# Weight sums and alpha*h rows moved between VectorE and GpSimd in a hybrid S5 and gMLP encoder layer

## The chip, the core and the metric

The kernel runs on one core of a Trainium2 chip. The metric is the time of one execution in microseconds of the device, and the time of a kernel is the median of its runs. The profile is of one further execution. TensorE does the matrix products, VectorE and GpSimd do elementwise work, ScalarE does activations and copies, and the queues of SyncE and ScalarE issue the transfers between device memory and the on-chip buffers.

## The reference

One layer of width 1024 over 2048 positions, all in float32, with `D_FF` 2816 and `ALPHA` the fourth root of 2:

```
h = layer_norm(x, emb_ln_g, emb_ln_b)
z = h @ w_in
y_ssm = s5_mixer(z[..., :512], ...)          # diagonal state space layer, GELU, GLU
y_sgu = sgu_mixer(z[..., 512:], ...)         # gated mixing inside blocks of 128 positions
mix = concat([rms_norm(y_ssm), rms_norm(y_sgu)]) @ w_out
h = layer_norm(ALPHA * h + mix, ln1_g, ln1_b)
ffn = (silu(h @ w_gate) * (h @ w_up)) @ w_down
ple = (p @ w_ple) * sigmoid(h @ w_ple_gate + b_ple_gate)
h = layer_norm(ALPHA * h + ffn + ple, ln2_g, ln2_b)
```

## The kernel before

Every product of float32 matrices is made of three passes. An operand is split into a rounded high part, which ScalarE casts (line 64), and the low rest, which VectorE subtracts (line 65); `mm3` then issues high times high (line 69), high times low (line 70) and low times high (line 71), each with 512 columns. So a tile of weights is usable after a load, a cast on ScalarE and a subtraction on VectorE. Raw loads go through three buffers (`raw`), split weights through six (`wsp`), and the pools `hT` and `hTx` hold 14 tiles each.

The work that the change touches lies between the end of the GLU and the start of the gated feed-forward network.

`glu` ends with the scaled rows of the state space branch (line 912), which are stored to `md`. Before its last step it starts the first output projection, `out_proj(0)`, which multiplies four tiles of 128 rows by the left half of `w_out`. When `glu` is done, its memory is freed, and the pool `pb` of `phase_b` is laid over it.

`mixed` then goes over four sets `tg` of 512 rows. For each set it loads the normalized input rows into four tiles `acc` (eight exist), scales them (line 1043), adds the output projection of two column halves (line 1061), takes the statistics (line 116), normalizes in place (line 299), and lets TensorE transpose eight column blocks (line 143). ScalarE writes the transposed rows with gain and bias (line 1071) to `hfd`. After that GpSimd turns the four `acc` tiles into `alpha*h`: for each column half it multiplies by `ALPHA*ln1_g` (line 1083) and adds `ALPHA*ln1_b` (line 1084), 16 instructions a set, from one buffer `S` that is loaded for each half and scaled by ScalarE (line 1080). SyncE stores the result to `xnd` (line 1086). The output projection of set `tg+1` is issued inside set `tg`, so that TensorE has work while VectorE normalizes. The split tiles of `w_out` are kept for all four sets: `keep` gives 14 tiles of `hTx` and two of `ff`.

Between the sets, `gate_sums` makes for one or two of four row groups the four sums of blocks of `w_ple_gate` that a seven-product scheme (Strassen and Winograd) needs: four loads into `tx` (line 1110; six tiles exist), four GpSimd instructions (lines 1111 to 1114) and four stores to `pgd` (line 1116). `operands(0)` loads the first block of transposed rows (block 0 is sets 0 and 1, block 1 is sets 2 and 3), splits it, and makes for each of four `j` the sums of it on GpSimd (`sums_B`, lines 1347 to 1350). `ple` runs the seven products of the gate of the per-layer embedding; product 2 and later ones read the sums, and its results go into eight new `acc` tiles (line 1199), whose memory is that of the sets' tiles once these are stored. Set 3 is cut in two: the first half is before the first products of `ple`, the statistics and everything after them follow its second product.

Then each of the two blocks runs 11 steps of `gate` and `up` (seven products each, with weight sums on GpSimd in `ops_A`, lines 1362 to 1369), and the products of `down`. In these steps `residual` reads `xnd` back and adds it to the accumulators on GpSimd (line 1243), two tiles a step in eight of the steps. In block 0 the steps also hold `down_sums`, four GpSimd instructions each (lines 1126 to 1129).

Each engine executes its own instructions in the order that a planner wrote before the run: it walks through the program by priority (earlier in the program goes first) and puts on each engine what is ready by its own estimate of durations. In the run, an engine or a queue whose next instruction waits does not go past it.

Of the kernel before, what the change touches and what calls it, by code (L numbers as in the profile page):

```python
# [7 lines left out]
F32 = mybir.dt.float32  # L8
# [3 lines left out]
ALU = mybir.AluOpType  # L12

P = 128
# [10 lines left out]
ALPHA = 2.0 ** 0.25  # L25
# [25 lines left out]
class Kern:  # L51
# [903 lines left out]
    def w_out(self, hf, k, t0):  # L955


        if (hf, k) not in self.wres:
            src = self.a["w_out"][0].rearrange("(k p) c -> p k c", p=P)
            k0 = k - k % 2  # L960
            r = self.load_w(src[:, k0:k0 + 2, hf * 512:(hf + 1) * 512], 1024)
            for i in range(2):
                w = self.keep() if hf or t0 else self.wspt()
                self.split(w[:, 0], w[:, 1], r[:, i * 512:(i + 1) * 512])
                self.wres[hf, k0 + i] = w
        return self.wres[hf, k] if hf or t0 else self.wres.pop((hf, k))

    def keep(self):
        self.kept += 1
# [3 lines left out]
    def phase_b(self, ctx):  # L973
        pb = self.pb = ctx.enter_context(self.tc.tile_pool(name="pb", bufs=1))
        a = self.a
        w_g = a["w_ffn_gate"][0].rearrange("(k p) c -> p k c", p=P)
        w_u = a["w_ffn_up"][0].rearrange("(k p) c -> p k c", p=P)
        mixed = self.mixed()
        for tg in range(3):
            next(mixed)  # L980
            self.gate_sums((tg, 3) if tg == 0 else (tg,))
        B = self.operands(0)
        next(B)
        next(mixed)
        tail = iter(())
        for blk in range(2):
            accs = [[None] * 4, [None] * 4]
            ple = self.ple(blk, B, accs)
            if blk == 0:
                next(ple)  # L990
                for _ in B:
                    pass
                next(ple)
                for _ in mixed:
                    pass
            for _ in ple:
                next(tail, None)

            rest = self.residual(blk, accs)
            for i in range(NP):  # L1000
                f = self.gate(w_g, i, self.B)
                if i:
                    next(rest, None)
                if blk == 0:
                    self.down_sums(i)
                self.up(blk, w_u, i, self.B, f)
            B = self.operands(1) if blk == 0 else iter(())
            tail = self.norm_out(blk, accs)
            for _ in self.down(blk, accs, tail):
                next(B, None)  # L1010
            for _ in B:
                pass
        for _ in tail:
            pass

    def mixed(self):


        nc, a = self.nc, self.a
        v = nc.vector  # L1020
# [16 lines left out]
        for tg in range(4):  # L1037
            c0 = tg * 512
            acc = []
            for t in range(4):  # L1040
                x = self.acct()
                nc.sync.dma_start(out=x, in_=self.h0d[c0 + t * P:c0 + (t + 1) * P, :])
                v.tensor_tensor(out=x, in0=x, in1=ag0, op=ALU.mult)
                acc.append(x)
            if tg == 0:
                op, ps0 = self.op0, self.op0_ps
                bias(ps0, 0)
                cps = [self.t512() for _ in range(4)]
                for t in range(4):
                    nc.scalar.copy(out=cps[t], in_=ps0[t])  # L1050
                pss = [cps, bias(next(op), 1)]
            else:
                pss = [bias(next(nxt), 0), ps1]
            if tg < 3:
                nxt = self.out_proj(c0 + 512)
                next(nxt)
                ps1 = bias(next(nxt), 1)
            for hf in ((0, 1) if tg == 0 else (1, 0)):
                for t in range(4):
                    xs = acc[t][:, hf * 512:(hf + 1) * 512]  # L1060
                    v.tensor_tensor(out=xs, in0=xs, in1=pss[hf][t], op=ALU.add)
            if tg == 3:
                yield
            mv = self.ln_stats(acc, D)
            rs = self.ln_rstd(mv)
            for t in range(4):
                self.normalize(acc[t], mv[:, t, 0:1], rs[:, t:t + 1])
            for k in range(8):
                ps = self.transpose4(acc, k * P)
                f = self.t512()  # L1070
                nc.scalar.activation(out=f, in_=ps, func=AF.Identity, scale=self.g1[:, k:k + 1],
                                     bias=self.b1[:, k:k + 1])
                nc.scalar.dma_start(out=self.hfd[tg, k * P:(k + 1) * P, :], in_=f)

            for hf in range(2):
                cs = slice(hf * 512, (hf + 1) * 512)
                gb = self.stile()
                for i, nm in enumerate(("ln1_g", "ln1_b")):
                    nc.sync.dma_start(out=gb[:, i], in_=a[nm][0][cs].unsqueeze(0).broadcast_to([P, 512]))
                nc.scalar.mul(gb, gb, ALPHA)  # L1080
                for t in range(4):
                    xs = acc[t][:, cs]
                    nc.gpsimd.tensor_tensor(out=xs, in0=xs, in1=gb[:, 0], op=ALU.mult)  # L1083
                    nc.gpsimd.tensor_tensor(out=xs, in0=xs, in1=gb[:, 1], op=ALU.add)  # L1084
            for t in range(4):
                nc.sync.dma_start(out=self.xnd[c0 + t * P:c0 + (t + 1) * P, :], in_=acc[t])
            yield

    def operands(self, blk):

        B = self.B = [[None] * 4 for _ in range(7)]
        for k in range(8):
            B[k // 4][k % 4] = self.split_f(self.load_f(blk, 0, k), self.hxt())
            if k == 3 and blk:
                yield
        yield
        for j in range(4):
            B[2][j] = self.split_f(self.load_f(blk, 1, j + 4), self.hxt())
            self.sums_B(blk, B, j)
            if blk:  # L1100
                yield

    def gate_sums(self, kks):

        g = self.nc.gpsimd
        W = self.a["w_ple_gate"][0].rearrange("(j k p) c -> k p j c", j=2, p=P)
        for kk in kks:
            a11, a12, a21, a22 = x = [self.txt() for _ in range(4)]
# [123 lines left out]

    def residual(self, blk, accs):

        for tg in range(2):
            for t in range(4):
                for hf in range(2):
                    cs = slice(hf * 512, (hf + 1) * 512)
                    x = self.txt()
                    r0 = blk * 1024 + tg * 512 + t * P  # L1240
                    self.nc.sync.dma_start(out=x, in_=self.xnd[r0:r0 + P, cs])
                    xs = accs[tg][t][:, cs]
                    self.nc.gpsimd.tensor_tensor(out=xs, in0=xs, in1=x, op=ALU.add)
                yield

    def rows(self, src, scale):

# [278 lines left out]
```

## Time and profile before

| | |
|---|---|
| median of 3 runs | 2327.17 us (2325.92 to 2329.01) |
| the profiled execution | 2327.55 us, with a span of 2325.8 us |
| TensorE matmul busy | 2171.2 us (93% of the span) |
| VectorE busy | 1555.5 us (67%) |
| ScalarE busy | 879.7 us (38%) |
| GpSimd busy | 734.6 us (32%) |
| mean granted TensorE clock | 0.97 |

The profiled execution is 1.75 us longer than its span; the sums further down are made against its own time. PE is TensorE, DVE is VectorE, ACT is ScalarE, POOL is GpSimd, and SPq, ACTq are queues that issue transfers. A busy share is an average over stages with different limits, so the stage around the change is read by itself.

### The profile page before, as it was taken

What the parts mean: (1) busy time and instruction counts of PE and PEld (TensorE: products, weight loads), DVE (VectorE), ACT (ScalarE), POOL (GpSimd) and SP (SyncE); (2) the same over time, 40 slices, a digit from 0 to 9 for tenths busy, and PEclk for the clock granted to TensorE, in tenths of its full rate; (3) what the DMA queues carried; (4) which work ended last, traced back from release to release, by engine and by line L of the source; (5) the groups of instructions that cost most, each with busy time, mean ns of one, the idle gap of its engine ahead of it and who ended that gap; (6) DMA issues with size and microseconds to landing.
All of it is one profiled execution on the core that took longest, in us unless ns stands there. A gap on an engine that the chain in (4) does not pass through costs nothing.

```text
span 2325.8 us, 27952 instructions
## 1 busy us (share of the span) xinstructions
PE 2171.2 (93%) x9556; PEld 1768.9 (76%) x9556; DVE 1555.5 (67%) x2672; ACT 879.7 (38%) x1503; POOL 734.6 (32%) x650
## 2 busy tenths in 40 slices
PE   7899998998799789999999989989999999999996
PEld 6677887766677567888888768868788888878885
DVE  7997779787465646666666676574566666565559
ACT  4434554442223433323232444434333332324442
POOL 1187100002535514645454330043134343410004
PEclk9999999999899899999999999989999999999998
DMA  8547445546765343454544666643233333336563
GB/s 265 148 141 244 122 136 155 147 127 232 254 238 200 128 138 133 166 173 166 173 167 164 227 212 209 196 151 130 82 105 127 106 126 116 107 130 214 194 197 134
DMA packets 312427, 382.66 MB, mean 165 GB/s; under 512 B 62246, under 2 KB 180054, under 8 KB 312284
## 3 DMA queue, kind: packets, MB, share of 16 engines
q1 hardware_dynamic: 261116, 315.30, 42.1%
q10 hardware_dynamic: 50080, 61.36, 7.5%
q0 software_dynamic: 1088, 4.21, 0.5%
q8 instruction: 75, 1.23, 0.2%
q14 instruction: 68, 0.56, 0.1%
HBM read 270.16 MB, written 110.64 MB: 164 GB/s over the span
## 4 chain that ended last, share of the span: by engine, by line
PE 65%; DVE 13%; DMA 7%; issue 7%; POOL 6%; ACT 1%; SPq 1%; POOLq 0%; ACTq 0%; DVEq 0%
PE ps L69 21%; PE ps L70 21%; PE ps L71 21%; DVE st L116 2%; POOL acc L1083 1%; DMA tx<-hfd 1%; POOL acc L1084 1%; DVE wsp L65 1%; PE ps L143 1%; DMA raw<-in_w_out_dram 1%; DVE hTx L65 1%; DVE z L912 1%; DMA raw<-in_w_ple_gate_dram 1%; POOL acc L1292 1%; DMA raw<-md 0%
## 5 line engine op out<-in xcount | busy, mean ns | idle before, releaser
L65 DVE TENSOR_TENSOR wsp<-raw,wsp 128x512 fp32r<-128x512 f32 x459 | 395.3, 868 | 293.4 <-ACT wsp L64 287.9
L64 ACT CAST wsp<-raw 128x512 fp32r<-128x512 f32 x469 | 287.6, 622 | 550.1 <-PE ps L71 320.0
L69 PE MATMUL ps<-hT,wsp 128*128 128x512 f32 x744 | 290.8, 391 | 6.1 <-ACT hT L312 6.1
L70 PE MATMUL ps<-hT,wsp 128*128 128x512 f32 x744 | 290.6, 391 | 1.0 <-DVE hT L313 1.0
L71 PE MATMUL ps<-hT,wsp 128*128 128x512 f32 x744 | 290.3, 390 | 0.0
L69 PE MATMUL ps<-wsp,ff 128*128 128x512 f32 x636 | 254.0, 399 | 20.9 <-ACT ff L64 20.9
L71 PE MATMUL ps<-wsp,ff 128*128 128x512 f32 x636 | 252.6, 399 | 5.6 <-DVE ff L65 5.4
L70 PE MATMUL ps<-wsp,ff 128*128 128x512 f32 x636 | 253.2, 398 | 0.2 <-DVE wsp L65 0.2
L69 PE MATMUL ps<-hTx,wsp 128*128 128x512 f32 x616 | 241.0, 391 | 3.7 <-DVE tx L1395 3.7
L70 PE MATMUL ps<-hTx,wsp 128*128 128x512 f32 x616 | 239.8, 389 | 0.0
L71 PE MATMUL ps<-hTx,wsp 128*128 128x512 f32 x616 | 239.7, 389 | 0.0
L1362 POOL TENSOR_TENSOR S<-raw 128x512 f32<-128x512 f32 x44 | 68.3, 1553 | 388.5 <-DVE wsp L65 279.4
L64 ACT CAST wsp<-S 128x512 fp32r<-128x512 f32 x158 | 97.9, 620 | 240.5 <-PE ps L71 164.3
L70 PE MATMUL ps<-wsp,hT 128*128 128x512 f32 x400 | 159.2, 398 | 15.0 <-DVE wsp L65 15.0
L69 PE MATMUL ps<-wsp,hT 128*128 128x512 f32 x400 | 160.7, 402 | 7.4 <-ACT acc L1199 5.5
L69 PEld LDWEIGHTS ps<-hT,wsp 128*128 128x128 f32 x744 | 140.3, 189 | 35.4 <-ACT hT L312 6.5
L70 PEld LDWEIGHTS ps<-hT,wsp 128*128 128x128 f32 x744 | 140.2, 188 | 31.0 <-DVE hT L313 2.3
L71 PEld LDWEIGHTS ps<-hT,wsp 128*128 128x128 f32 x744 | 140.2, 188 | 29.1
L1292 POOL TENSOR_TENSOR acc<-acc,t 128x512 f32<-128x512 f32 x24 | 36.3, 1530 | 399.1 <-ACT acc L1286 399.1
L65 DVE TENSOR_TENSOR wsp<-S,wsp 128x512 fp32r<-128x512 f32 x158 | 122.8, 777 | 56.5 <-ACT wsp L64 54.3
L69 PEld LDWEIGHTS ps<-wsp,ff 128*128 128x128 f32 x636 | 122.7, 193 | 49.4 <-ACT ff L64 24.0
L71 PE MATMUL ps<-wsp,hT 128*128 128x512 f32 x400 | 158.3, 396 | 0.0
(342 smaller groups left out, 4344.4 us busy)
## 6 DMA issues: line engine op xcount, KB each, us to landing
raw<-fod SPq DMA_DIRECT2D x126, 256.0 KB
raw<-in_w_in_dram SPq DMA_DIRECT2D x48, 512.0 KB
raw<-in_w_ffn_gate_dram SPq DMA_DIRECT2D x44, 512.0 KB
raw<-in_w_ffn_up_dram SPq DMA_DIRECT2D x44, 512.0 KB
fod<-tx ACTq DMA_DIRECT2D x88, 256.0 KB
raw<-wtd SPq DMA_DIRECT2D x72, 256.0 KB
fod<-ff ACTq DMA_DIRECT2D x66, 256.0 KB
tx<-hfd SPq DMA_DIRECT2D x56, 256.0 KB
```

Of the source, the lines that this page charges most:

```text
L64: nc.scalar.copy(out=hi, in_=src)
L65: (e or nc.vector).tensor_tensor(out=lo, in0=src, in1=hi.bitcast(F32), op=ALU.subtract)
L69: mm(ps, lhsT=lh, rhs=rh, start=start, stop=False, skip_group_check=more)
L70: mm(ps, lhsT=lh, rhs=rl, start=False, stop=False, skip_group_check=more)
L71: mm(ps, lhsT=ll, rhs=rh, start=False, stop=stop, skip_group_check=more)
L116: nc.vector.bn_stats(out=st[:, c, :], in_=t[:, c * 512:(c + 1) * 512])
L143: self.nc.tensor.transpose(ps[:, t * P:(t + 1) * P], x[:, col:col + P], self.ident)
L912: v.scalar_tensor_tensor(out=mx[:, ct, :].rearrange("p (c s) -> p s c", s=L), in0=yT[ct].rearrange("p (s c) -> p s c", s=L), scalar=self.g ...
L1083: nc.gpsimd.tensor_tensor(out=xs, in0=xs, in1=gb[:, 0], op=ALU.mult)
L1084: nc.gpsimd.tensor_tensor(out=xs, in0=xs, in1=gb[:, 1], op=ALU.add)
L1292: nc.gpsimd.tensor_tensor(out=xh, in0=xh, in1=gb[0][hf], op=ALU.mult)
L1362: g.tensor_tensor(out=s1, in0=a21, in1=a22, op=ALU.add)
```

## The change

It has five parts.

1. `gate_sums` runs its four sums on VectorE instead of GpSimd, 16 instructions in all.
2. In `mixed`, sets 0 and 1 have their gain and bias (32 instructions) on VectorE. Sets 2 and 3 have none: their normalized rows are stored to `xnd` as they are, without the loads into `S`.
3. `residual` of block 1 makes up for it: in each of its eight steps it loads gain and bias for 512 columns into an `ff` tile, scales them on ScalarE, and multiplies and adds on GpSimd before the addition that was there. The steps go over two row tiles and one column half each, in place of one row tile and two halves.
4. `operands` yields after each `j` in both blocks, and `phase_b` takes one more step of it, so that the split and the sums for `j` 0 stand in the program before set 3.
5. Of the right half of `w_out`, the tiles `k` 4 to 7 are split into `wsp` for set 0 and not kept. Set 1 loads and splits them again and keeps them. `keep` still hands out 16 tiles.

```diff
-                w = self.keep() if hf or t0 else self.wspt()
+                w = self.keep() if t0 or (hf and k < 4) else self.wspt()
...
-        return self.wres[hf, k] if hf or t0 else self.wres.pop((hf, k))
+        return self.wres[hf, k] if t0 or (hf and k < 4) else self.wres.pop((hf, k))
...
         B = self.operands(0)
         next(B)
+        next(B)
         next(mixed)
...
-            for hf in range(2):
+            for hf in range(2 if tg < 2 else 0):
...
-                    nc.gpsimd.tensor_tensor(out=xs, in0=xs, in1=gb[:, 0], op=ALU.mult)
-                    nc.gpsimd.tensor_tensor(out=xs, in0=xs, in1=gb[:, 1], op=ALU.add)
+                    v.tensor_tensor(out=xs, in0=xs, in1=gb[:, 0], op=ALU.mult)
+                    v.tensor_tensor(out=xs, in0=xs, in1=gb[:, 1], op=ALU.add)
...
             self.sums_B(blk, B, j)
-            if blk:
-                yield
+            yield
...
     def gate_sums(self, kks):
-        g = self.nc.gpsimd
+        g = self.nc.vector
...
     def residual(self, blk, accs):
+        nc, g, a = self.nc, self.nc.gpsimd, self.a
         for tg in range(2):
-            for t in range(4):
+            for t0 in (0, 2):
                 for hf in range(2):
                     cs = slice(hf * 512, (hf + 1) * 512)
-                    x = self.txt()
-                    r0 = blk * 1024 + tg * 512 + t * P
-                    self.nc.sync.dma_start(out=x, in_=self.xnd[r0:r0 + P, cs])
-                    xs = accs[tg][t][:, cs]
-                    self.nc.gpsimd.tensor_tensor(out=xs, in0=xs, in1=x, op=ALU.add)
-                yield
+                    if blk:
+                        gb = self.fft(F32)
+                        for i, nm in enumerate(("ln1_g", "ln1_b")):
+                            nc.sync.dma_start(out=gb[:, i],
+                                              in_=a[nm][0][cs].unsqueeze(0).broadcast_to([P, 512]))
+                        nc.scalar.mul(gb, gb, ALPHA)
+                    for t in (t0, t0 + 1):
+                        x = self.txt()
+                        r0 = blk * 1024 + tg * 512 + t * P
+                        nc.sync.dma_start(out=x, in_=self.xnd[r0:r0 + P, cs])
+                        if blk:
+                            g.tensor_tensor(out=x, in0=x, in1=gb[:, 0], op=ALU.mult)
+                            g.tensor_tensor(out=x, in0=x, in1=gb[:, 1], op=ALU.add)
+                        xs = accs[tg][t][:, cs]
+                        g.tensor_tensor(out=xs, in0=xs, in1=x, op=ALU.add)
+                    yield
```

## Rows read from the trace of the kernel before

**Rows 1.** Windows: us, busy PE, PEld, DVE, ACT, POOL (xcount); PEclk, DMA share, GB/s.

```profile
530.00:890.00 360.00, 305.76 (x1301) 242.81 (x1301) 209.66 (x304) 119.41 (x191) 150.26 (x107) 0.91 0.58 197
...
540.00:600.00 60.00, 49.02 (x216) 38.94 (x214) 50.82 (x64) 17.75 (x30) 24.48 (x15) 0.93 0.72 249
...
890.00:1298.00 408.00, 404.29 (x1771) 331.37 (x1771) 264.27 (x335) 130.91 (x216) 207.58 (x140) 1.00 0.49 163
...
1660.00:2088.00 428.00, 427.93 (x1886) 353.92 (x1884) 266.18 (x358) 135.93 (x223) 147.86 (x100) 1.00 0.34 111
```

**Rows 2.** TensorE's waits, 530 to 890 us: us in total, times, longest us.

```profile
PE ps L143 <- ACT t L1071: 11.4, 1, 11.4
PE ps L70 <- DVE wsp L65: 9.6, 3, 8.4
PE ps L69 <- ACT hTx L64: 7.4, 1, 7.4
PE ps L143 <- DVE acc L299: 7.3, 8, 3.7
PE ps L69 <- ACT acc L1199: 5.5, 3, 4.1
PE ps L143 <- DVE acc L1190: 5.2, 1, 5.2
```

**Rows 3.** Timeline of TensorE (start us, us, what): first and last of ten matmuls.

```profile
537.50 0.77 PE L69 MATMUL ps<-hTx,hT 128*128 128x512 f32 x1 [7.40 <-ACT hTx L64]
...
541.60 0.40 PE L69 MATMUL ps<-hTx,hT 128*128 128x512 f32 x1
```

**Rows 4.** Timeline of SyncE's queue, five of its rows.

```profile
524.86 1.04 SPq L266 DMA_DIRECT2D raw<-in_w_out_dram  x2
...
576.65 4.47 SPq L1116 DMA_DIRECT2D pgd<-tx  x4
...
582.21 1.44 SPq L266 DMA_DIRECT2D raw<-in_w_out_dram  x3
...
625.35 7.00 SPq L1086 DMA_DIRECT2D xnd<-acc  x4
632.44 2.41 SPq L944 DMA_DIRECT2D raw<-md  x3
```

**Rows 5.** Timeline of GpSimd: second weight sums, first and last; end of set 0's rows.

```profile
572.96 1.29 POOL L1111 TENSOR_TENSOR tx<-tx 128x512 f32<-128x512 f32 x1 [6.68 <-DMA tx<-in_w_ple_gate_dram]
...
578.08 2.22 POOL L1114 TENSOR_TENSOR tx<-tx 128x512 f32<-128x512 f32 x1
...
629.47 2.53 POOL L1084 TENSOR_TENSOR acc<-acc,S 128x512 f32<-128x512 f32 x2
```

**Rows 6.** Timeline of ScalarE: casts before line 1071 and after the sums; a late copy.

```profile
599.11 0.62 ACT L64 CAST hT<-raw 128x512 fp32r<-128x512 f32 x1 [1.88 <-DMA raw<-md]
...
778.10 0.62 ACT L64 CAST hTx<-tx 128x512 fp32r<-128x512 f32 x1 [1.05 <-POOL tx L1350]
...
821.74 1.07 ACT L1199 COPY acc<-ps 128x512 f32<-128x512 f32 x2 [3.49 <-DMA xnd<-acc]
```

**Rows 7.** Timeline of VectorE: the same instruction alone, beside GpSimd, and late.

```profile
530.13 3.97 DVE L912 SCALAR_TENSOR_TENSOR z<-yT,chv,ps 128x512 f32<-128x512 f32 x4 [1.88 <-PE ps L909]
...
549.90 2.48 DVE L65 TENSOR_TENSOR hTx<-raw,hTx 128x512 fp32r<-128x512 f32 x4
...
588.88 10.12 DVE L65 TENSOR_TENSOR hTx<-raw,hTx 128x512 fp32r<-128x512 f32 x6 [0.89 <-ACT hTx L64]
...
637.88 1.43 DVE L65 TENSOR_TENSOR hT<-raw,hT 128x512 fp32r<-128x512 f32 x2 [10.76 <-ACT hT L64]
```

**Rows 8.** GpSimd by line (L1243: block 1): busy us, mean ns, idle before, releasers.

```profile
L1083 POOL TENSOR_TENSOR acc<-acc,S 128x512 f32<-128x512 f32 x32 | 45.9, 1455 | 60.7 <-PE ps L143 46.0 <-ACT S L1080 14.7
...
L1243 POOL TENSOR_TENSOR acc<-acc,tx 128x512 f32<-128x512 f32 x16 | 23.8, 1507 | 44.8 <-DMA tx<-xnd 44.8
...
L1111 POOL TENSOR_TENSOR tx<-tx 128x512 f32<-128x512 f32 x4 | 5.1, 1283 | 41.5 <-DMA raw<-md 21.7 <-DMA tx<-in_w_ple_gate_dram 10.0 <-DMA hfd<-t 9.8
```

## Prediction

> **What bounds the kernel now.** I read the windows first, to see which stretch TensorE loses, then its waits there, then the timelines of the queues that it waited on.
>
> TensorE is busy for 427.93 of 428 us in block 1's steps, but only for 305.76 of 360 us between the end of the GLU and the feed-forward network [rows 1]. These 54.2 us of idleness are almost all that this change can reach. Six kinds of wait hold 46.4 of them [rows 2]. Idleness costs a little more than itself: the granted clock is 0.91 in this stretch against 1.00 in the steps [rows 1], and after the wait of 7.4 us ten matmuls start within 4.10 us, nine intervals of 0.456 us [rows 3], where a full stretch has 428/1886 = 0.227 us [rows 1]. That is the lower of the two clock levels, and 9 x 0.229 = 2.1 us lost after one long wait.
>
> Traced back, the waits lead to GpSimd and to the SyncE queue that waits for it.
>
> - 7.4 us: set 0's second half needs split weights in `hTx`, memory that is free only when the GLU is through. Their loads were issued at 524.86 [rows 4], 12.6 us before TensorE starts at 537.50 [rows 3].
> - 11.4 us: set 0's transposes wait for line 1071 on ScalarE, which stands behind a cast at 599.11 that waited for a load [rows 6]. The loads of `w_out` before it left at 582.21, behind four stores of weight sums [rows 4], whose last GpSimd instruction ended at 580.30 [rows 5].
> - 7.3 us: the normalizations of sets 1 and 2. For set 1, VectorE stood still for 10.76 us before a split [rows 7]; its load left at 632.44, behind stores of `alpha*h` [rows 4] whose rows GpSimd finished at 632.00 [rows 5].
> - 9.6 and 5.2 us: `ple` waits for a weight split behind the last sums of `operands`, cast at 778.10 right after line 1350 [rows 6], and for set 3's normalization, behind those sums' splits on VectorE.
> - 5.5 us: copies into `acc` wait for the store of set 3's `alpha*h` [rows 2, 6].
>
> **The change, part by part.** *Durations.* On GpSimd an instruction of the moved kind takes 1.455 us [rows 8]. VectorE's subtraction, of the same shape and with two on-chip inputs, takes 2.48/4 = 0.62 us alone and 10.12/6 = 1.69 us beside GpSimd [rows 7]. I take 0.62 for moved work, since GpSimd then has little left beside it; 1.69 is the other bound.
>
> The Trainium skill (Perfetto Trace Analysis, Optimizing Scalar/DVE Operations) warns that moving work between VectorE and GpSimd might not help, because they share an SBUF read port. The rows show the sharing (0.62 against 1.69 us), but also that the work takes less than half as long on VectorE; by the rule the sum would be the 2311.6 of the first rival, by the rows it is the one below.
>
> *Weight sums (1) and set 0's first half (5).* The second set's four sums fall from 7.34 us (572.96 to 580.30 [rows 5]) to 4 x 0.62 = 2.5, and the first set's, at the mean, from 4 x 1.455 = 5.8 to 2.5. Both lie in the chain of loads, sums, stores and loads of `w_out`: 4.8 + 3.3 = 8.1 us earlier. The last load of `w_out` follows the second of the six subtractions that took 1.69 us each beside GpSimd: 2 x 1.07 = 2.1 more. So line 1071 comes 10 us sooner. TensorE's own arrival moves by enough: with weights in `wsp` it need not wait for 537.5, only for the first subtraction behind line 912, which ends at 534.1 [rows 7], or earlier, and then 48 x 0.227 = 10.9 us of products cover the time until the memory is free. Bounds: 0, if the loads are as late as now; 7.4 + 11.4 + 2 x 2.1 = 23.0, if both waits vanish. I take **10**, the shorter chain's.
>
> VectorE must hold it: it is busy for 50.82 of 60 us there [rows 1]. Added are 8 sums and 16 rows of set 0 (24 x 0.62 = 14.9 us, some after 600) and four splits (2.5); the subtractions freed from GpSimd give back 6.4 us and others like them more. It stays near full, which is why I don't take more than 10.
>
> *Rows of sets 0 and 1 on VectorE (2).* 16 x 1.455 = 23.3 us on GpSimd become 9.9 on VectorE, so the stores of `xnd`, and the loads that are queued behind them, leave some 10 us sooner; that covers VectorE's 10.76 us, and with it the normalizations' wait: 7.3 + 2.1 at most, 0 at least. I take **7**. The wait for the gain buffer (line 1080) moves to VectorE; queued behind it are splits, line 1061 and the next statistics, on which TensorE waits.
>
> *No rows for sets 2 and 3, and an earlier `j` 0 (2, 4).* GpSimd's 23.3 us of set 2 lie among its sums, which end that much sooner; TensorE comes 17 us sooner, so 6.3 of the 8.4 us wait go. Part 4 puts `j` 0's five loads, casts and subtractions and four sums ahead of set 3's on SyncE, ScalarE, VectorE and GpSimd; the splits end before set 3's statistics, and the 5.2 go. With half a slow clock after them, 1.5: **13**, from 5 to 14.8 + 2.1 = 16.9. Set 3's store leaves right after its transposes instead of behind 23.3 us of rows: 5.5 + 2.1 at most, **6**, at least 0. Four loads into `S` are saved on SyncE.
>
> *Block 1's residual (3).* 32 more GpSimd instructions of 1.507 us [rows 8], 48 us, in a GpSimd that is busy for 147.86 of 428 us [rows 1]. No TensorE wait is visible there now. Each step also issues two gain loads on SyncE, ahead of `ops_A`'s weight loads, and a scaling on ScalarE, ahead of casts that feed TensorE. Block 0, with `down_sums`' four instructions beside its residual's two, is the nearest row with six a step: 408/1771 against 428/1886 is 0.2304 against 0.2269 us a matmul, 0.58 us in a step of 168. Eight steps: 4.7 at most, 0 at least; I take **2**, as there are two fewer loads and stores of 512 KB than `down_sums` has.
>
> *Reload (5).* Two loads of 512 KB, 1.05 MB, at 197 GB/s [rows 1] are 5.3 us if nothing hides them; four casts and splits stand beside 21.8 us of products (96 x 0.227). I take **1**; 0 to 5.3.
>
> *Sum.* Against the profiled execution's 2327.55 us (span 2325.8 and 1.75 around it; 0.4 above the median of the runs): 10 + 7 + 13 + 6 = 36 gained, 3 lost, 2327.55 - 33 = **2294.6 us**. All bounds together: 2327.55 - 56.9 = 2271 and 2327.55 - 5 + 10 = 2333.
>
> **The rivals.** *VectorE inherits the waits (22%).* Sets 0 and 1 gain nothing, because VectorE now stands where GpSimd stood and its other work stands behind it; the 10 and the 7 are lost, the 13, the 6 and the 3 stay: 2327.55 - 16 = 2311.6. For it: 50.82 of 60 us busy [rows 1]. Against it: 150.3 idle us of VectorE over the stretch (360 - 209.66), and instructions that become half as long. It is the time that the page's rule above would give too.
>
> *Slower (10%).* The same place, more strongly: GpSimd waited 41.5 us before its weight sums, for loads and stores, and 60.7 before its rows, half of them for sets 0 and 1 [rows 8]. Together 71.9 us of waiting now belong to VectorE's queue, in front of the splits and normalizations that feed TensorE. When more than 33 us of them fall where VectorE had work, the kernel gets slower; at two thirds, 47.9, it takes 2294.6 + 47.9 = 2342. Against it: the planner places them when it believes the data there, and VectorE has 150 us to spare.
>
> *Nothing comes of it (8%).* TensorE waits for transfers instead, and what it saves on GpSimd it loses on loads: within 4.7 us of now. Against it: 360 us at 197 GB/s are 70.9 MB at a DMA share of 0.58 [rows 1]; at full share they need 209 us.
>
> *More (10%).* ScalarE's order changes, so that line 1071 no longer stands behind casts: the 10 become 23, the others reach their upper bounds, 2271 to 2282.
>
> **How the numbers follow.** My forecast, 2282 to 2303, has 50%; the likeliest single time is 2294.6. The range adds most of the first rival and part of the last: 2273 to 2319. About 0.2%, 4.7 us, is what a measurement of this kernel can tell from no change. Faster: 50 + 22 + 10 = 82%; same 8%; slower 10%.
>
> **What would show it.** In the changed profile, TensorE's idle time in this stretch (54.2 us) falls to about 25; the waits of 7.4 us for `hTx` and 5.5 for `acc` are gone; VectorE's subtractions there take 0.62 us, hardly any 1.69; the steps of block 1 still show 0.227 to 0.231 us a matmul. I would be wrong if VectorE shows long idle times before lines 1083 or 1111 with TensorE waiting behind them, if line 1071 still comes at 599, or if waits in block 1's steps exceed 5 us.

## The result, and the profile after

The changed kernel takes **2289.35 us** (median of 4 runs, 2284.58 to 2296.08); the kernel before took 2328.09 us beside it (4 runs, 2325.92 to 2329.27). The ratio is 0.9835, with a 95% interval from 0.981 to 0.9859: 38 us less, where 33 were forecast. The profiled execution took 2291.72 us, its span is 2289.9 us (before: 2325.8).

The windows of the changed kernel, in the columns of [rows 1]; the second stretch is block 1's steps.

```profile
530.00:890.00 360.00, 335.08 (x1470) 269.15 (x1469) 231.68 (x384) 131.66 (x211) 46.85 (x35) 0.96 0.60 205
1622.00:2050.00 428.00, 426.05 (x1874) 351.13 (x1873) 278.15 (x354) 143.97 (x231) 199.20 (x133) 1.00 0.37 120
```

Against [rows 1] TensorE's idle time between 530 and 890 us has fallen from 54.2 to 360 - 335.08 = 24.9 us, GpSimd's work there from 150 to 47 us, and the granted clock has risen from 0.91 to 0.96. What TensorE still waits for there (us in total, times, longest):

```profile
PE ps L143 <- DVE acc L1190: 7.1, 1, 7.1
PE ps L69 <- ACT t L1072: 4.6, 2, 2.4
PE ps L69 <- DVE z L912: 3.5, 1, 3.5
PE ps L143 <- DVE acc L299: 3.1, 7, 0.8
PE ps L69 <- ACT ff L64: 3.1, 2, 2.1
PE ps L70 <- DVE wsp L65: 1.8, 1, 1.8
PE ps L143 <- ACT t L1072: 1.6, 2, 1.0
```

Line 1071 of before is line 1072 here. Of [rows 2], the 7.4 us for `hTx` (3.5 us for line 912 stand in their place) and the 5.5 us for copies into `acc` are gone, the 11.4 us for line 1071 have become 4.6 + 1.6, the 7.3 us for the normalizations 3.1 and the 9.6 us for `wsp` 1.8. The wait at line 1190 has grown, from 5.2 to 7.1 us.

To see where the time came from, I follow five points that both kernels pass: the first of the bias matmuls that close the products of set 1's right half, of the left halves of sets 1, 2 and 3, and of the second product of `ple`. From set 1 on, the right half comes first. First before, then after (start us, us, what):

```profile
585.93 0.49 PE L1032 MATMUL ps<-ff,one 33*128 33x512 f32 x1
...
629.72 0.49 PE L1032 MATMUL ps<-ff,one 33*128 33x512 f32 x1
...
684.49 0.73 PE L1032 MATMUL ps<-ff,one 33*128 33x512 f32 x2
...
741.99 0.49 PE L1032 MATMUL ps<-ff,one 33*128 33x512 f32 x1
...
835.02 1.20 PE L1183 MATMUL ps<-ff,one 33*128 33x512 f32 x4
```

```profile
582.91 0.49 PE L1033 MATMUL ps<-ff,one 33*128 33x512 f32 x1
...
623.27 0.96 PE L1033 MATMUL ps<-ff,one 33*128 33x512 f32 x3
...
674.86 0.49 PE L1033 MATMUL ps<-ff,one 33*128 33x512 f32 x1
...
724.57 0.73 PE L1033 MATMUL ps<-ff,one 33*128 33x512 f32 x2
...
797.54 0.73 PE L1183 MATMUL ps<-ff,one 33*128 33x512 f32 x2
```

The lead grows from 3.0 to 6.5, 9.6, 17.4 and 37.5 us. At the end of the span it is 35.9, so later work, block 1 with it, gives 1.6 back.

The table has the same distances for every run: A from set 1's right half to its left one, B to set 2's left half, C to set 3's, D to `ple`'s second product. "Start" is the first of the five points. Two kernels with the same code up to there differ by 2.2 us in it (586.73 and 584.51), so a difference of that size in one profile says nothing; B, too, is 51.6, 55.1 and 54.9 us in three kernels that differ only behind it in the program (after, no early `j` 0, rows of sets 2, 3 on VectorE). The last column is the median of the timed runs.

| run | start | A | B | C | D | median us |
|---|---|---|---|---|---|---|
| before | 585.9 | 43.8 | 54.8 | 57.5 | 93.0 | 2328.1 |
| after | 582.9 | 40.4 | 51.6 | 49.7 | 73.0 | 2289.4 |
| sums on GpSimd again | 581.5 | 48.9 | 49.7 | 49.7 | 71.5 | 2298.3 |
| rows on GpSimd again | 583.1 | 40.6 | 60.7 | 57.4 | 70.1 | 2306.2 |
| no early `j` 0 | 581.8 | 42.7 | 55.1 | 49.7 | 71.6 | 2292.1 |
| part 5 undone | 586.7 | 32.0 | 49.7 | 49.7 | 71.0 | 2281.2 |
| reload only | 588.8 | 34.6 | 49.7 | 49.7 | 71.8 | 2286.2 |
| rows of sets 2, 3 on VectorE | 581.9 | 41.3 | 54.9 | 54.9 | 70.4 | 2293.6 |
| part 5 undone, set 3 normalized first | 584.5 | 33.8 | 49.7 | 49.7 | 64.8 | 2274.5 |
| useless products that hold `S` | 581.1 | 41.7 | 65.5 | 49.7 | 72.6 | 2303.8 |
| useless products, `S` free | 581.4 | 40.4 | 56.0 | 49.7 | 73.0 | 2291.9 |
| sums alone (on before) | 588.0 | 26.6 | 62.5 | 57.8 | 90.9 | 2318.9 |
| rows 2, 3 dropped alone (on before) | 587.1 | 42.8 | 56.5 | 57.7 | 71.9 | 2309.7 |
| part 5 alone (on before) | 581.4 | 49.5 | 56.5 | 58.0 | 90.7 | 2330.3 |

### The profile page after: what moved, and what is told of

Read it like the earlier page. It is cut to its first block, busy times and chain, and to the rows that moved or that the text cites. A ratio compares the mean times of both kernels' runs of the same rounds, so it can differ in the third digit from the quotient of the medians.

```text
span 2289.9 us, 27942 instructions
## 1 busy us (share of the span) xinstructions
PE 2160.6 (94%) x9556; PEld 1762.1 (77%) x9556; DVE 1569.8 (69%) x2724; ACT 887.6 (39%) x1511; POOL 671.6 (29%) x602
## 4 chain that ended last, share of the span: by engine, by line
PE 66%; DVE 14%; DMA 8%; issue 7%; POOL 3%; ACT 2%; SPq 0%; ACTq 0%; DVEq 0%; POOLq 0%
PE ps L69 21%; PE ps L70 21%; PE ps L71 21%; DMA tx<-hfd 1%; DVE st L116 1%; DVE wsp L65 1%; DMA raw<-md 1%; PE ps L143 1%; DVE z L912 1%; DMA U<-ud 1%; DVE hTx L65 1%; POOL acc L1303 1%; DVE hT L65 1%; DVE acc L1044 1%; POOL acc L1304 0%
## 5 line engine op out<-in xcount | busy, mean ns | idle before, releaser
L70 PE MATMUL ps<-wsp,hT 128*128 128x512 f32 x416 | 165.1, 397 | 6.0 <-DVE wsp L65 6.0
L69 PE MATMUL ps<-wsp,hT 128*128 128x512 f32 x416 | 165.8, 399 | 4.8 <-DVE z L912 4.8
L65 DVE TENSOR_TENSOR wsp<-S,wsp 128x512 fp32r<-128x512 f32 x158 | 129.7, 821 | 56.3 <-ACT wsp L64 54.3
L71 PE MATMUL ps<-wsp,hT 128*128 128x512 f32 x416 | 164.5, 395 | 0.0
L69 PEld LDWEIGHTS ps<-wsp,ff 128*128 128x128 f32 x636 | 121.6, 191 | 48.9 <-ACT ff L64 24.2
```

Source lines behind the costliest of these rows:

```text
L65: (e or nc.vector).tensor_tensor(out=lo, in0=src, in1=hi.bitcast(F32), op=ALU.subtract)
L69: mm(ps, lhsT=lh, rhs=rh, start=start, stop=False, skip_group_check=more)
L70: mm(ps, lhsT=lh, rhs=rl, start=False, stop=False, skip_group_check=more)
L71: mm(ps, lhsT=ll, rhs=rh, start=False, stop=stop, skip_group_check=more)
```

## Experiments

### One part undone at a time

Four kernels, each the changed one with a part undone. The weight sums on GpSimd again:

```
 def gate_sums(self, kks):
-    g = self.nc.vector
+    g = self.nc.gpsimd
```

> The changed kernel with the weight sums back on GpSimd, all else as changed. Queue theory (SyncE's stores and loads wait for whoever computes, and GpSimd takes longer): the stretch of set 0 loses most of the 6.5 us that it gained, time 2293 to 2298 us, and line 1072 of set 0 comes later than 590. Shared-port rival (a move between the two engines buys nothing): within 2 us of the changed kernel's 2289.

2298.32 us (2291.47 to 2300.56); ratio to before 0.9872 [0.9857, 0.9888]. So the sums on VectorE are worth 9 us between the medians where the other parts are in; the intervals just touch (the changed kernel's ends at 0.9859). The table puts the loss into A (48.9 against 40.4 us); B and D give some of it back. The profiled execution is the fastest of its runs, 7 us below their median, so its A is rather too short.

The rows of sets 0 and 1 on GpSimd again:

```
-                    v.tensor_tensor(out=xs, in0=xs, in1=gb[:, 0], op=ALU.mult)
-                    v.tensor_tensor(out=xs, in0=xs, in1=gb[:, 1], op=ALU.add)
+                    nc.gpsimd.tensor_tensor(out=xs, in0=xs, in1=gb[:, 0], op=ALU.mult)
+                    nc.gpsimd.tensor_tensor(out=xs, in0=xs, in1=gb[:, 1], op=ALU.add)
```

> The changed kernel with the rows of sets 0 and 1 back on GpSimd. Queue theory: the stores of alpha*h hold SyncE's queue again, the waits for the normalizations of sets 1 and 2 return, 7 to 11 us, time 2296 to 2301. Shared-port rival: within 2 us of 2289. A third view, that the loss of these rows from GpSimd only matters through VectorE's slower instructions beside it: subtractions near 1.7 us return, but TensorE's waits don't.

2306.18 us (2302.55 to 2308.74); ratio 0.991 [0.9896, 0.9923]: 16.8 us, more than I had expected of them. GpSimd's timeline in this kernel, first and last rows of sets 0 and 1:

```profile
590.89 3.50 POOL L1084 TENSOR_TENSOR acc<-acc,S 128x512 f32<-128x512 f32 x2 [51.76 <-PE ps L143]
...
621.30 2.98 POOL L1085 TENSOR_TENSOR acc<-acc,S 128x512 f32<-128x512 f32 x2
660.17 2.51 POOL L1084 TENSOR_TENSOR acc<-acc,S 128x512 f32<-128x512 f32 x2 [35.89 <-PE ps L143]
...
684.07 2.98 POOL L1085 TENSOR_TENSOR acc<-acc,S 128x512 f32<-128x512 f32 x2
```

And TensorE's longest group of waits there:

```profile
PE ps L143 <- DVE acc L299: 14.7, 12, 7.1
```

Set 0's rows end at 624.3 us, and the stores and the `md` loads that stand behind them on SyncE leave from 616.27 and 624.72 us on. With the rows on VectorE, in the changed kernel, they end at 610.7, and stores and loads leave from 610.11 and 613.42. TensorE pays at the next normalizations: B and C are 9.1 and 7.7 us longer; D is 2.9 us shorter, and the two profiled executions differ by 13.4 us.

The sums of `j` 0 where they were:

```
         next(B)
-        next(B)
```

> The changed kernel without the earlier step of the operand sums. If the 20 us at the sums of the operands come from GpSimd's rows of set 2 being gone, little is lost: 2289 to 2293. If they come from the new order, 2297 or more, with a wait of TensorE for a weight split behind the last sums.

2292.1 us (2290.48 to 2293.46); ratio 0.985 [0.9837, 0.9864]. That is 2.75 us above the changed kernel, which the intervals don't separate from nothing. D, where part 4 should show, is 71.6 us without it and 73.0 with it; the longer distance in this profile is B, before part 4 comes in. The wait of 7.1 us at `ple`'s line 1190 (here 1189) is there without part 4 too.

Part 5 undone, so that all of `w_out`'s right half stays in SBUF:

```
-                w = self.keep() if t0 or (hf and k < 4) else self.wspt()
+                w = self.keep() if hf or t0 else self.wspt()
...
-        return self.wres[hf, k] if t0 or (hf and k < 4) else self.wres.pop((hf, k))
+        return self.wres[hf, k] if hf or t0 else self.wres.pop((hf, k))
```

> The changed kernel with the first four tiles of the right half of w_out kept as before, no reload. The wait of 7.4 us for hTx returns. If the chain through the loads of w_out sets the end of set 0's stretch, as the prediction says, the time is 2289 to 2292; if TensorE's own arrival sets it, 2292 to 2296.

**2281.18 us** (2279.27 to 2282.24); ratio 0.9804 [0.979, 0.9817]: 8.2 us faster than with part 5. The intervals overlap a little, from 0.981 to 0.9817, but all five runs lie below all four of the changed kernel. Both views missed. Its waits, 525 to 860 us, the first and the two at line 1072:

```profile
PE ps L69 <- ACT hTx L64: 7.4, 1, 7.4
...
PE ps L143 <- ACT t L1072: 2.6, 2, 2.0
PE ps L69 <- ACT t L1072: 1.4, 1, 1.4
```

The 7.4 us for `hTx` are back, and the kernel is faster all the same: it comes to the "start" point some 4 us later, and to set 1's left half 4.6 us earlier (618.68 against 623.27). The windows show where. Two of them in this kernel, then the same two in the changed one (columns as in [rows 1]):

```profile
592.00:602.00 10.00, 7.78 (x35) 5.53 (x36) 9.90 (x17) 5.13 (x8) 0.00 (x0) 1.00 0.96 343
602.00:612.00 10.00, 10.00 (x45) 8.26 (x45) 8.51 (x15) 2.79 (x5) 0.00 (x0) 1.00 0.97 337
```

```profile
592.00:602.00 10.00, 4.76 (x19) 3.03 (x18) 8.69 (x15) 3.55 (x5) 0.00 (x0) 0.76 0.98 328
602.00:612.00 10.00, 10.00 (x41) 8.13 (x41) 8.98 (x15) 4.04 (x7) 0.00 (x0) 0.90 0.90 328
```

The DMA share is 0.90 to 0.98 in both; little is free there to hide 1.05 MB. In the changed kernel TensorE arrives early, stands idle for 5.2 of 10 us, and has a granted clock of 0.76 and 0.90, where this one has 1.00. It waits for line 1072 there, which itself waits for the stores to `hfd` of the tiles that it writes: 5.0 us from 582 to 630 in the changed kernel, 4.4 in this one, 8.0 in the next run, which has the second load and not the early start.

### What part 5 costs, and what the early start brings

The second load alone; set 0's products wait for `hTx` again:

```
-                w = self.keep() if t0 or (hf and k < 4) else self.wspt()
+                w = self.keep() if t0 or (hf and k < 4) else self.hxt() if hf else self.wspt()
```

> The changed kernel, except that the weights of set 0's right half for k 4 to 7 go into hTx again; they are still loaded a second time for set 1. Theory: the second load of 1.05 MB, in a stretch whose DMA share is already 0.84 to 0.92, is what part 5 costs, so the cost stays and the 7.4 us wait for hTx comes back: set 1's left half ends at 623 us or later, 2287 to 2296 us. Rival: the use of the two wsp buffers for set 0 (order of the buffers, an earlier start) is what costs, and it goes with this edit: 2279 to 2284 us, like the kernel that keeps w_out.

2286.21 us (2284.24 to 2287.44); ratio 0.9821 [0.9807, 0.9834]: just below the range of the theory, and above the rival's. The second load, with the four casts and splits that come with it, costs 2286.2 - 2281.2 = 5.0 us between the medians; the intervals overlap from 0.9807 to 0.9817, but no run of one lies among those of the other. In the table A is 2.6 us longer than with part 5 undone. The same two windows as above:

```profile
592.00:602.00 10.00, 5.72 (x29) 3.99 (x29) 8.51 (x15) 3.64 (x7) 0.00 (x0) 0.91 0.84 306
602.00:612.00 10.00, 9.98 (x34) 8.01 (x35) 6.97 (x11) 5.32 (x8) 0.00 (x0) 0.75 0.97 333
```

The idle time (4.3 of 10 us) and the low clock (0.91, then 0.75) are here without the early start, so the early start is not their cause. The other 3 us of the 8.2 would belong to the early start, but the intervals of this run and of the changed kernel overlap. By the profiles the early start gains nothing: set 1's left half ends at 623.41 us here and at 623.27 there, although TensorE passes the start point 5.9 us apart, more than the 2.2 that profiles differ by.

Part 5 alone, the same two lines as above on the kernel before:

> The kernel before with part 5 alone: w_out's right half for k 4 to 7 goes through the wsp buffers in set 0 and is loaded again for set 1. Theory, from the kernel that keeps w_out: the early start of set 0 gains some 3 us up to the end of the right halves, and set 1's left half, whose end is set by late weight sums and weights, takes it back, with the second load on top: 2327 to 2333 us. Rival: on the kernel before, the wait of 7.4 us for hTx is a gain by itself, as the prediction had it: 2322 to 2325 us.

2330.27 us (11 runs, 2325.48 to 2334.29); ratio 1.0017 [1.0008, 1.0026]: a little slower, as expected. In its profile, the fastest of the 11 runs, the start point comes 4.6 us sooner and A is 5.7 us longer.

### The other parts alone, on the kernel before

The weight sums alone on VectorE (the edit of the first run, the other way round):

> The kernel before with the weight sums alone moved to VectorE. Theory: the sums' part is that which the kernel without part 5 showed up to set 1's left half, 11 us, and nothing later takes it back: 2314 to 2319 us. Rival: with the rows still behind them on GpSimd, what comes early is waited for at the normalizations of the next sets: 2321 to 2327 us.

2318.9 us (2316.79 to 2319.52); ratio 0.9966 [0.9954, 0.9978]. The total is as expected, the way there is not: A is 17.2 us shorter, not 11, and B takes 7.7 us back. Its longest group of waits, 525 to 885 us:

```profile
PE ps L143 <- DVE acc L299: 12.0, 8, 6.9
```

With the rows still on GpSimd, the normalization of set 1 is late, as the rival said; it takes a part, not all. Compare 7.3 us for it in [rows 2].

No rows for sets 2 and 3, done in block 1's residual instead, alone:

```
-            for hf in range(2):
+            for hf in range(2 if tg < 2 else 0):
...
+                        if blk:
+                            g.tensor_tensor(out=x, in0=x, in1=gb[:, 0], op=ALU.mult)
+                            g.tensor_tensor(out=x, in0=x, in1=gb[:, 1], op=ALU.add)
```

> The kernel before with one part alone: sets 2 and 3 of block 1 have no rows of alpha*h in the stretch, the residual does them on GpSimd in block 1; rows of sets 0 and 1 and the weight sums stay on GpSimd, and the sums of j 0 stay where they were. Theory: GpSimd's queue loses 32 instructions of 1.45 us ahead of the operand sums, so the waits behind it go: some 13 us less, 2 back in block 1: 2313 to 2319 us. Rival: the rows of sets 0 and 1 and the weight sums, still on GpSimd, keep VectorE's two-input work slow and the normalizations late, and set the time: 2321 to 2327 us.

2309.72 us (2304.61 to 2310.99); ratio 0.9924 [0.9912, 0.9936]: 17.5 us, the largest single part and more than expected. All of it is in D, 21.1 us shorter, while A, B and C stay within 1.7 us of before. Its waits keep what belongs to the sets before, and the 9.6 us for `wsp` and the 5.5 us for `acc` of [rows 2] are gone:

```profile
PE ps L143 <- ACT t L1071: 11.5, 1, 11.5
PE ps L143 <- DVE acc L299: 8.2, 8, 3.8
PE ps L69 <- ACT hTx L64: 7.4, 1, 7.4
PE ps L143 <- DVE acc L1190: 7.1, 1, 7.1
```

The single gains, 8.4 us for the sums and 17.5 for the dropped rows, less 3.0 for part 5, add up to 22.9 us of 38. The rows of sets 0 and 1 are worth 16.8 us when the other parts are in; alone on the kernel before they were not run, so what they bring by themselves is not shown.

Is it the leaving out, or only the engine? The changed kernel with all rows in place, sets 2 and 3 on VectorE too, and a plain residual:

```
-            for hf in range(2 if tg < 2 else 0):
+            for hf in range(2):
...
-                        if blk:
+                        if False:
                             g.tensor_tensor(out=x, in0=x, in1=gb[:, 0], op=ALU.mult)
```

> The changed kernel, except that sets 2 and 3 have their rows of alpha*h too, on VectorE (16 more two-input instructions each), and block 1's residual adds without them. Theory: VectorE is busy for some 20 us more between 660 and 790 us, where the sums of the operands and the normalizations stand in the same queue, and part of it is on the path; block 1 gives 2 us back: 2292 to 2299 us. Rival: it fits in VectorE's idle time, and it is the engine alone that counts, not the leaving out: 2286 to 2290 us.

2293.59 us (2287.97 to 2294.7); ratio 0.9844 [0.983, 0.9857]. Most of the gain, then, is that GpSimd is rid of the rows. This run is 4 us above the changed kernel, with intervals that overlap, so the medians don't show that VectorE's being spared them brings anything more. In the table C is 5.2 us longer, where every other kernel with the rows of sets 0 and 1 on VectorE has 49.7, and D 2.6 shorter; B, 3.3 us longer, lies before these rows.

### Sharing, or standing in a queue?

The changed kernel with useless products on GpSimd beside VectorE's rows:

```
                     v.tensor_tensor(out=xs, in0=xs, in1=gb[:, 1], op=ALU.add)
+                    for i in range(8):
+                        nc.gpsimd.tensor_tensor(out=scr, in0=gb[:, i // 4, i % 4 * P:(i % 4 + 1) * P],
+                                                in1=scr, op=ALU.mult)
```

> The changed kernel with eight more 128-column products on GpSimd beside each of the 16 VectorE pairs of the rows of sets 0 and 1; they read the scaled rows and write a scratch that nothing reads. Theory: what made the rows on GpSimd cost 17 us was that others waited for their results and stood behind them in its queue; with nothing waiting for it, GpSimd's work costs 0 to 5 us through VectorE's two-input instructions that take longer beside it: 2289 to 2294 us. Rival: the two engines' sharing is the cost, whoever waits: 2299 us or more.

2303.84 us (2298.58 to 2305.95); ratio 0.9894 [0.9881, 0.9908], as the rival had it. But the trace shows that something did wait for these products. Timelines of GpSimd, ScalarE and VectorE in this kernel (the added lines shift its numbers: 1083 is the scaling, 1086 and 1087 are the rows, 1089 the products):

```profile
605.71 22.30 POOL L1089 TENSOR_TENSOR scr<-S,scr 128x128 f32<-128x128 f32 x32 [31.60 <-DMA hfd<-t]
...
633.62 1.06 ACT L1083 ACTIVATE S<-S 128x1024 f32<-128x1024 f32 x1 [12.65 <-DMA S<-in_ln_b_dram]
...
635.22 0.69 DVE L65 TENSOR_TENSOR hT<-raw,hT 128x512 fp32r<-128x512 f32 x1 [12.91 <-ACT hT L64]
```

They read the scaled gains in `S`, of which there is one buffer. It was free at 628 us, its refill landed at 633.6, ScalarE stood before its scaling for 12.65 us with casts behind it, and VectorE for 12.91 us behind those casts; in the table all of the loss is in B, 13.9 us. The run measures a queue more than the sharing. So once more, with products that hold `S` only at the start of each group:

```
-                                                in0=gb[:, i // 4, i % 4 * P:(i % 4 + 1) * P]
+                                                in0=scr if t + i else gb[:, 0, 0:P]
```

> As the run with the useless products on GpSimd, but they read and write the scratch alone, except for the first one of each group of four row tiles; so the one buffer of scaled gains is not held by them, and ScalarE does not stand behind its refill as it did there (12.9 us). Theory: without that queue the two engines' sharing costs 0 to 6 us: 2287 to 2295 us. Rival: sharing is the cost, the 2304 us of the run before come again: 2299 us or more.

2291.93 us (2290.97 to 2294.64); ratio 0.9852 [0.9839, 0.9864]. VectorE and GpSimd by line, 540 to 720 us (busy us, mean ns, idle before), the rows and their company:

```profile
L1087 DVE TENSOR_TENSOR acc<-acc,S 128x512 f32<-128x512 f32 x16 | 11.9, 783 | 0.0
L1086 DVE TENSOR_TENSOR acc<-acc,S 128x512 f32<-128x512 f32 x16 | 11.6, 768 | 6.4 <-ACT S L1083 5.3 <-DMA hfd<-t 1.0
...
L1089 POOL TENSOR_TENSOR scr<-scr 128x128 f32<-128x128 f32 x124 | 69.9, 564 | 9.7
```

VectorE's rows take 0.77 to 0.78 us in place of 0.68, with 74 us of GpSimd work beside this stretch, and the kernel is 2.6 us slower, which the intervals don't separate from nothing. So of the 14.5 us in the run before, the buffer accounts for some 12; its rows took 0.79 and 0.82 us, so a little of that can be sharing.

This test doesn't weigh the sharing at the strength that the rows on GpSimd had. By line, 540 to 720 us, VectorE's subtractions, sums and rows together take some 6 us longer here than in the changed kernel; with the rows of sets 0 and 1 on GpSimd the subtractions and sums take some 14 us longer (`hT<-raw` 0.85 us each instead of 0.69, lines 1113 and 1114 1.20 instead of 0.69). In that run VectorE also stood idle before the `hT<-raw` splits for 30.2 us instead of 16.0. So the queue seems the larger part, but how much of the 16.8 us is sharing stays open.

### A version that beats both

Part 5 undone, and set 3's statistics and normalization put ahead of the operands of `j` 1 to 3 in the program (those of `j` 0 stand before set 3 in either order, and the sums themselves are GpSimd's; VectorE splits their results):

```
-            if tg == 3:
-                yield
             mv = self.ln_stats(acc, D)
             rs = self.ln_rstd(mv)
             for t in range(4):
                 self.normalize(acc[t], mv[:, t, 0:1], rs[:, t:t + 1])
+            if tg == 3:
+                yield
```

> The kernel that keeps w_out in SBUF (part 5 undone, 2281 us), with set 3's statistics and normalization ahead of the sums of the operands of j 0 and 1 in VectorE's order. Theory: the 7.1 us wait for the normalized sets behind those sums shrinks to 2 to 3 us and the sums have slack until the first products are read: 2275 to 2279 us. Rival: the sums, later by the same time, are waited for by the first products in place of it: 2280 to 2284 us.

**2274.5 us** (2272.95 to 2275.5); ratio 0.9771 [0.9757, 0.9784], 6.7 us below the kernel with part 5 undone and 15 below the changed one, with intervals that don't overlap, and half a us below the expected range. VectorE's timeline there, from set 3's statistics to the first sums of `ple`:

```profile
727.67 1.27 DVE L116 BATCH_NORM_STATS2 st<-acc 128x6 f32<-128x512 f32 x2
...
732.04 0.67 DVE L65 TENSOR_TENSOR hT<-tx,hT 128x512 fp32r<-128x512 f32 x1
...
741.42 2.98 DVE L299 TENSOR_SCALAR acc<-acc,mv,rs 128x1024 f32<-128x1024 f32 x4
...
745.51 2.47 DVE L1190 TENSOR_TENSOR acc<-acc,ps 128x512 f32<-128x512 f32 x4
```

and with part 5 undone alone:

```profile
727.85 4.08 DVE L65 TENSOR_TENSOR hT<-tx,hT 128x512 fp32r<-128x512 f32 x3
731.86 1.78 DVE L65 TENSOR_TENSOR hTx<-tx,hTx 128x512 fp32r<-128x512 f32 x1
733.55 2.38 DVE L65 TENSOR_TENSOR hT<-tx,hT 128x512 fp32r<-128x512 f32 x2
...
745.96 2.98 DVE L299 TENSOR_SCALAR acc<-acc,mv,rs 128x1024 f32<-128x1024 f32 x4
```

From set 3's left half (717.68 and 718.10 us) the normalization ends 26.7 us later here and 30.8 us there. The wait of 7.1 us at line 1190 is gone, one wait for a split in `wsp` is 2.2 us instead of 0.5, and D is 6.2 us shorter than with part 5 undone.

The way there is not the one forecast. The same twelve splits stand between line 1062 and the normalization in both kernels. With part 5 undone alone, the first six take 8.2 us beside GpSimd's last sums, which run until 734.8; here the statistics come first, at the same duration in both, and the splits follow when those sums are almost over, at 0.63 to 0.69 us each. All twelve take 8.1 us instead of 12.2, and that is the 4.1 us between 30.8 and 26.7. So by these rows the gain came from what runs beside GpSimd's work, the sharing that the useless products had shown as small.

## Why the prediction held, step by step

**What bounds the kernel.** Right. The gain is in the stretch of 54.2 idle us, and it came by way of the queues that the prediction traced: GpSimd's, and SyncE's behind it.

**Weight sums and set 0's first half, 10 us.** Mis-sized, as the sum of a gain and a loss. Line 1072 on ScalarE starts where the chain said, some 9 us before the cast of [rows 6]:

```profile
590.30 1.45 ACT L1072 ACTIVATE t<-ps,chv 128x512 f32<-128x512 f32 x2
```

But the lead at set 1's left half is 6.5 us, where 10 less 1 were forecast. The failing step is part 5's: "with weights in `wsp` it need not wait", and **1** us for the reload. TensorE waited 3.5 us for line 912 instead of 7.4 for `hTx`, and gained 3 us at the start point by the profiles; what it then waited for, line 1072 behind stores of transposed rows, came no sooner, and the second load of 1.05 MB cost some 5 us. The mean rate of 197 GB/s of [rows 1] gave the right upper bound (5.3); the value of 1 came from looking at casts, splits and products for cover, and not at the DMA share of the 20 us in which the load falls. Without part 5, the lead at set 1's left half would have been 629.72 - 618.68 = 11.0 us. The sums by themselves were probably under-sized too: alone they shorten A by 17.2 us, though B takes 7.7 us of it back. The prediction counted two groups of four sums; GpSimd did two more in this stretch, from 605.10 and 620.29 us in the trace of before, among set 0's rows.

**Rows of sets 0 and 1, 7 us.** Under-sized. The two sets after set 1's left half take (684.49 - 629.72) + (741.99 - 684.49) = 112.3 us before and 101.3 after: 11.0 us, above the bound of 9.4, and 16.8 us when this part alone is undone. The bound was that of the normalizations' wait in the profile of before. It is no bound when another part lets TensorE arrive earlier: the run with the sums alone shows that same wait at 12.0 us. With the reload's 1 us the two terms are 16 by the prediction; the lead at set 3's left half is 17.4 us, so the errors nearly cancel, which is luck.

**No rows for sets 2 and 3, early `j` 0, and the copies, 13 + 6 us.** Right as a sum: D is 20.1 us shorter, and the run with the dropped rows alone has 21.1, so it is the rows. What part 4 adds is not measurable. The terms are not right: set 3's 5.2 us, which the 13 counted on, did not go but became 7.1. They are 7.1 without part 4 as well (the run without the early `j` 0, and the one with the rows dropped alone), so the early step is not the reason; set 3's normalization stands behind splits that run beside GpSimd's sums, and the last run got the wait back. What made up for it is the clock. The windows of D, before and after:

```profile
742.00:835.00 93.00, 70.19 (x281) 53.30 (x280) 51.34 (x70) 34.92 (x59) 46.53 (x33) 0.85 0.47 165
724.60:797.50 72.90, 64.02 (x281) 51.91 (x280) 39.02 (x65) 30.73 (x52) 11.64 (x8) 0.93 0.43 148
```

Idle time falls from 22.8 to 8.9 us, and the same 281 matmuls are busy for 6.2 us less, where the forecast had some 2 us for the clock. That the sum still fits is in part luck.

**Block 1, 2 us.** Right. 37.5 us of lead shrink to 35.9, TensorE's idle time in the steps is 1.95 us, and a matmul takes 428/1874 = 0.228 us, within the forecast 0.227 to 0.231. From `ple`'s second product to the end the changed kernel takes 1492.4 us, the kernel before 1490.8, and the run with the plain residual 1489.6; single profiles don't separate these.

**The rivals.** *VectorE inherits the waits* did not come about: VectorE stood before its rows for 6.0 us in all, 0.9 of it before the first three halves; GpSimd had stood for 60.7 before the rows of all four sets [rows 8], 38.4 of it before those of sets 0 and 1, more than the half that the second rival took. By line, 540 to 660 us in the changed kernel:

```profile
L65 DVE TENSOR_TENSOR hT<-raw,hT 128x512 fp32r<-128x512 f32 x22 | 14.9, 687 | 16.0 <-ACT hT L64 15.9
...
L1084 DVE TENSOR_TENSOR acc<-acc,S 128x512 f32<-128x512 f32 x12 | 7.7, 683 | 0.9 <-DMA hfd<-t 0.9
L1085 DVE TENSOR_TENSOR acc<-acc,S 128x512 f32<-128x512 f32 x12 | 7.7, 682 | 0.0
```

Moved rows and split subtractions take 0.68 to 0.69 us there (the 0.62 of the prediction is the spacing of instructions that overlap a little), not the 1.69 of [rows 7]. Where GpSimd still works, they do get longer; the same kernel, 700 to 745 us:

```profile
L65 DVE TENSOR_TENSOR hT<-tx,hT 128x512 fp32r<-128x512 f32 x14 | 13.3, 996 | 9.5 <-ACT hT L64 9.5
L65 DVE TENSOR_TENSOR hTx<-tx,hTx 128x512 fp32r<-128x512 f32 x6 | 7.4, 1230 | 9.7 <-ACT hTx L64 9.7
```

The rule of the Trainium skill that was weighed ahead (Perfetto Trace Analysis, Optimizing Scalar/DVE Operations) says that a move between these two engines might not help. Here it did, by 9 us for the sums and 16.8 for the rows: the sharing that the page names is in the rows above, but where GpSimd is left without work no one shares. The run with useless work and hardly a queue puts the cost of that much sharing at 2.6 us between the medians; how much of the 16.8 was sharing it doesn't show, and the last run gained its 4.1 us by it. *Slower* fell with the first rival. *Nothing comes of it*, by way of transfers, was wrong for the whole and right for part 5.

## What to carry to other kernels

When work leaves a slow engine, price it by the queues that stand behind its results, and price several moves together: each moves the time at which the next wait begins, so a wait's length in the old profile bounds neither what one part brings nor what it costs. Before adding a load, read the DMA share of the very stretch in which it falls, not of the stage; an earlier start is worth only what the next thing waited for also comes earlier. An experiment with extra work must hold no buffer and no place in a queue that others need, or it measures those. And when a reordering helps, compare the durations of the same instructions in both orders before crediting the order: here they became shorter.

## What was not expected of the hardware

At a DMA share of 0.9 to 0.98, 328 to 343 GB/s, 1.05 MB more, with their casts and splits, cost 5.0 us of the kernel's time (2286.2 against 2281.2 us); 1.05 MB at 328 GB/s are 3.2 us. GpSimd's products of 128x128 took 0.564 us in the last run of that kind, those of 128x512 1.455 us [rows 8]: a quarter of the columns costs nearly four tenths of the time. VectorE's splits take 0.63 to 0.69 us when GpSimd is still and up to 1.78 beside its sums, while its statistics (line 116) take the same with and without them. And the lower clock went with TensorE's longer idle time, not with when it arrived: from 592 to 612 us the granted clock, whose levels are 1.2 and 2.4 GHz, is 0.76 and 0.90 in the changed kernel, which stood idle for 5.2 us, 0.91 and 0.75 in the run with the second load but no early start, which stood for 4.3, and 1.00 in both windows with part 5 undone, which stood for 2.2.
